# A backbone kernel on one core: the second layer's latent rows are loaded during the first layer's last expert, and that expert's rows are added to them on chip

## The chip, the cores and the metric

The kernel runs on one core of a Trainium2 chip. The metric is the device time of one execution in microseconds (us); lower is better.

## The reference

The model is a trunk of two layers over 512 latent rows and 256 context rows of 1024 numbers (float32). Each layer normalises and modulates its input, mixes it (attention, retention and a recurrence between an input and an output projection), adds the result to the residual, and then runs 16 experts. Each expert picks 64 latent rows and 32 context rows, and its results are added back to the rows that it picked. The second layer has no context output.

```python
    for i in range(DEPTH):                                   # DEPTH = 2
        ...
        hl = _modulate(_rms(xl, norm1_g[i]), sh1_l, sc1_l)
        hc = _modulate(_rms(xc, norm1_g[i]), sh1_c, sc1_c)
        mix_l, mix_c = _mixer(hl, hc, ...)                   # h @ w_in, heads, concat, @ w_out
        xl = xl + g1_l * mix_l
        xl = xl + g2_l * _expert_choice_ffn(_modulate(_rms(xl, norm2_g[i]), sh2_l, sc2_l), ...)
        if need_ctx:                                         # layer 0 only
            xc = xc + g1_c * mix_c
            xc = xc + g2_c * _expert_choice_ffn(...)
    return xl

def _expert_choice_ffn(h, router_w, w_gate, w_up, w_down):
    ...
    aff, idx = lax.top_k(jnp.swapaxes(probs, 1, 2), cap)     # each of 16 experts picks cap rows
    xs = h[bidx, idx]
    hid = jax.nn.silu(xs @ w_gate) * (xs @ w_up)             # per expert
    out = (hid @ w_down) * aff[..., None]
    return jnp.zeros_like(h).at[bidx, idx].add(out)
```

## The kernel before

`emit` (L1478) builds one program. For each layer it runs `mixer` (normalisation, input projection, heads), `outer` (output projection, residual, routing, gather of the first expert's rows) and `experts`, and then goes on to the next layer. The residual between the layers lies in DRAM, in `xr_l` (latent rows) and `xr_c` (context rows).

**The experts of layer 0.** `outer` writes the residual after the mixer to `xr_l` and `xr_c` (`base_write`). For each expert `gate_up` multiplies the gathered latent rows with two weight matrices (`gu`, L1304), `gate_up_c` does it for the context rows (`guc`, L1380), `down` (`oe`, L1457) and `down_c` (`oec`, L1470) multiply with the third, and `scatter` (L1403) adds the scaled results, `ob` (L1460) and `oc` (L1473), into `xr_l` and `xr_c` in DRAM by an indirect DMA on POOL's queue. `down_c` of an expert stands after `gate_up` of the next one; that of the last stands at the end of `experts`.

**The experts of layer 1** have latent rows only, and these are not scattered. The residual stays in SBUF; `onehot` (L1406) compares an `iota` row with the expert's indices (`oh`, L1409) and makes two copies of the result rows for the matmul (`obs`, L1415 on ACT, L1416 on DVE); `combine` (L1442) then multiplies the one with the other (`cb`, L1447), which puts each row at its place, and adds it to the residual (L1449).

**Between the layers.** After the last expert `mod_bulk` (L305) makes two of the next layer's modulation rows: four 2 MB tiles of `mod_w` are loaded (`mwt`, L314) and multiplied (`macc`, L317), the sums are added to `mrow` (L319), and the first row is turned (`mT`, L330) and copied into the columns `ab` (L339). Then layer 1's `load_x` (L375) loads four latent tiles `xl` and two context tiles `xc` of 512 KB each from `xr_l` and `xr_c` (L383). `norm1` (L386) squares them on ACT into a PSUM tile called `junk` (L398), scales them (L409 on DVE, L411 on ACT) and transposes them (`xT`, L420). The input projection loads its weights as `wraw` (L449, 512 KB), splits them into two parts `ws` (L456 on ACT, L457 on DVE) and multiplies with the split activations `hh` and `hl` (`pf`, `pt`, L462 to L464).

**What sets the order.** A tile scheduler orders the instructions of each engine; each engine then runs its list strictly in that order, and waits where an operand or a buffer is not ready. SP's queue carries nearly all loads, in a list of its own. The PE instructions of `experts` are kept in program order (`pe`, L1369). Expert weights, `mwt`, `xl` and `xc` share a ring of 2 MB buffers in three pools (`bigm`, `big` with 5, `bign`); a load waits until the tile that lay in its buffer has been used. PSUM tiles of one pool take its four banks in turn (`b`), so a new tile waits for the reader of the tile four places before.

```python
        xl = self.t("big", [4, D], "xl")                       # load_x
        for t, x in enumerate(xs):
            eng.dma_start(x, src_l[t * P:(t + 1) * P] if t < 4 else src_c[(t - 4) * P:(t - 3) * P])
        ...
        if ctx:
            late()                                             # experts: down_c of the last expert
        self.fixed = False
        if mn is not None:
            self.mod_bulk(mn, (2, 3))
```

Of the kernel before, what the change touches and what calls it, by code (L numbers as in the profile page):

```python
# [20 lines left out]
P = 128  # L21
L = 512
C = 256
T = L + C
D = 1024
KD = D // P
NE = 16
# [3 lines left out]
DEPTH = 2  # L31
# [36 lines left out]
class Trunk:  # L68
    def __init__(self, ctx, tc, a, out):
        self.tc = tc  # L70
        self.nc = tc.nc
        self.a = a
        self.out = out
        self.n = 0
        self.fl = 0
        self.nw = 0
        self.pools = {}
        self.late = []
        self.mj = 0
        self.fixed = False  # L80
        pool = lambda nme, **kw: ctx.enter_context(tc.tile_pool(name=nme, **kw))
        self.cp = pool("cst", bufs=1)
        self.sp = pool("small", bufs=2)
        self.dr = pool("dr", bufs=1, space=bass.MemoryType.DRAM)
        self.pools["big"] = pool("big", bufs=NBIG)
# [287 lines left out]
        return g2  # L373

    def load_x(self, src_l, src_c, eng, ctx=True):  # L375
        xl = self.t("big", [4, D], "xl")
        self.xt = [xl]
        xs = [xl[:, t] for t in range(4)]
        if ctx:
            xc = self.t("big", [2, D], "xc")  # L380
            xs += [xc[:, t] for t in range(2)]
        for t, x in enumerate(xs):
            eng.dma_start(x, src_l[t * P:(t + 1) * P] if t < 4 else src_c[(t - 4) * P:(t - 3) * P])  # L383
        return xs

# [728 lines left out]
    def route_(self, i, s, xs, lg, ssp, base):  # L1114
        nc = self.nc
# [31 lines left out]
        for t in range(nt):  # L1147
            h, u = divmod(t, nt // 2)
# [36 lines left out]
            nc.vector.tensor_copy(af[o], tt[:, 0])  # L1185
            nc.vector.tensor_scalar(sc[o], tt[:, 1], float(nq), float(q), op0=ALU.mult, op1=ALU.add)
        r = {"g": g, "af": af, "sc": sc}
        if i == DEPTH - 1:
            r["ix"] = self.cst([NE], nm="ixl")
            for q in range(nq):  # L1190
                nc.vector.tensor_copy(r["ix"][cap * q:cap * (q + 1)], tt[:, 1])
# [119 lines left out]
    def experts(self, i, m, mn, st, first, base_l, base_c):  # L1311
        nc = self.nc
        ctx = i < DEPTH - 1
        bl = base_l.rearrange("t (h e) -> (t h) e", h=2)
        bc = base_c.rearrange("t (h e) -> (t h) e", h=4) if ctx else None
        self.g2 = self.gate2(m, ctx)
        gl = lambda e: self.moe_gather(m, 0, self.xh_l[i], st[0]["g"][:, e // 2:e // 2 + 1])
        gc = lambda e: self.moe_gather(m, 1, self.xh_c, st[1]["g"][:, e // 4:e // 4 + 1])
        xl, W, hid = first
        if ctx:  # L1320
            xc = gc(0)()
        self.fixed = True
        late = None
        part = []
        if not ctx:
            self.iota = self.t("iota", [L], "iota")
            nc.sync.dma_start(self.iota, self.a["iota"])
        for e in range(NE):
            if e > 0:
                W = self.load_experts(i, e, 6 * e + 6)  # L1330
                hid = self.gate_up(e, W, xl)
            turn = []
            if e % 2 == 1 and e < NE - 1:
                turn.append(gl(e + 1))
            if ctx and e % 4 == 3 and e < NE - 1:
                turn.append(gc(e + 1))
            if late is not None:
                late()
            pair = len(part) == 2 or not ctx and e == NE - 1
            if pair:  # L1340
                self.combine(part, 0)
            self.turn_hid(hid)
            if turn:
                xl = turn[0]()
            if ctx:
                hc = self.gate_up_c(e, W, xc)
                if len(turn) > 1:
                    xc = turn[1]()
            elif pair:
                self.combine(part, 1)  # L1350
                part = []
            if not ctx and e == NE - 1:
                dd = self.keep_x((1, 3))
            ob = self.down(e, W, hid, st[0])
            if ctx:
                self.scatter(bl, ob, st[0], e)
                self.turn_hid_c(hc)
                late = lambda e=e, W=W, hc=hc: self.down_c(e, W, hc, st[1], bc)
            else:
                part.append(self.onehot(e, ob, st[0]))  # L1360
        if part:
            self.last(part[0], dd, base_l)
        if ctx:
            late()
        self.fixed = False
        if mn is not None:
            self.mod_bulk(mn, (2, 3))
# [110 lines left out]
def emit(ctx, tc, a, out):  # L1478
    k = Trunk(ctx, tc, a, out)
    k.consts()  # L1480
    ms = [k.mod_start(i) for i in range(DEPTH)]
    src = (a["x"], a["ctx"])
    for i in range(DEPTH):
        last = i == DEPTH - 1
        base = (out, None) if last else (k.xr_l, k.xr_c)
        with ExitStack() as cw:
            k.open(cw, k4=(NK4, 0))
            with ExitStack() as cr:
                k.open(cr, P=(2, 1), d=(2, 1), b=(2, 1))
                rr = cr.enter_context(ExitStack())  # L1490
                k.open(rr, "right", q2=(NQ2, 0), ring=(NRING, 0), w4=(NW4, 0), mw=(NMW, 0))
                with ExitStack() as ca:
                    k.open(ca, w6=(NW6, 0), st=(NST, 0), p=(NPT, 0))
                    xs, g1 = k.mixer(i, ms[i], None if last else ms[i + 1], src, src)
                k.open(cw, bigm=(NBIGM, 0), gathl=(1, 0), xsl=(2, 0))
                with ExitStack() as cb:
                    k.open(cb, x2=(NX2, 0), x1=(NX1, 0))
                    if not last:
                        k.open(cb, xc=(1, 0))

                    def free():
                        rr.close()
                        k.open(cw, "right", bign=(NBIGN[i], 0))

                    st, xl = k.outer(i, ms[i], xs, src[1], g1, free, *base)
            k.open(cw, ob=(2 if not last else 1, 0), g2=(2 if not last else 1, 0))
            if not last:
                k.open(cw, gathc=(1, 0), xsc=(2, 0), hidc=(2, 0), oc=(1, 0))
            else:
                k.open(cw, iota=(1, 0), oh=(2, 0), obs=(4, 0))  # L1510
            k.open(cw, b=(4, 1), d=(2, 1))
            k.experts(i, ms[i], None if last else ms[i + 1], st, xl, *base)
        src = base
# [91 lines left out]
```

## Time and profile before

| What | Value |
|---|---|
| Time, median of 3 runs (lowest to highest) | 1968.45 us (1968.3 to 1970.06) |
| Profiled execution, its own time | 1968.01 us |
| Its span, from first to last instruction | 1966.2 us |
| PE (matmul) busy | 1823.2 us, 93% |
| DVE busy | 869.5 us, 44% |
| ACT busy | 604.4 us, 31% |
| POOL busy | 94.1 us, 5% |
| DMA | 541.70 MB, mean 275 GB/s over the span |
| Mean granted TensorE clock | 0.98 of full speed |

Times in the trace count from the start of the span. The execution's own time is 1.8 us longer than its span. Layer 0's experts run from about 525 us to 1061 us, the passage to layer 1 lies between 1056 us and 1096 us, and layer 1's experts take the last quarter. A line of the timeline gives the start, the duration, the engine, the program line and the operation, with its output and inputs (`out<-in`); in brackets stands how long the engine had been idle before, and what released it.

### The profile page before, as it was taken

How to read it: one execution, taken by the hardware profiler on the slowest of the kernel's cores; microseconds unless marked ns; L12 is line 12 of the kernel's file. 1: busy time of each engine (PE TensorE's matmuls, PEld its weight loads, DVE VectorE, ACT ScalarE, POOL GpSimd, SP SyncE). 2: the span in 40 equal slices, each digit the busy share in tenths (PEclk: the TensorE clock that was granted, in tenths of full speed). 3: DMA queues.
4: the chain of work that ended last, by engine and by line, in shares of the span. 5: the costliest groups of instructions: out<-in, count | busy, mean ns of one | idle time of the engine just before them, and what ended most of it. 6: DMA issues, size and time to landing. Idle time of an engine off the chain costs nothing.

```text
span 1966.2 us, 28927 instructions
## 1 busy us (share of the span) xinstructions
PE 1823.2 (93%) x11972; PEld 1059.9 (54%) x11972; DVE 869.5 (44%) x2049; ACT 604.4 (31%) x1257; POOL 94.1 (5%) x102
## 2 busy tenths in 40 slices
PE   6999999999899999999997989999994998888887
PEld 5788888677533333333333779986671332332322
DVE  6797867575510111011101687976763221222212
ACT  5656456433210101011102485564431111110111
POOL 0000000000110111111001000000001000000000
PEclk9999999999999999999999999999996999999999
DMA  8453334236789999999999521111449999999996
GB/s 318 134 170 108 127 129 133 70 128 249 282 350 404 401 407 404 404 401 406 394 398 353 204 73 43 44 44 58 159 163 367 427 427 428 427 427 427 427 427 278
DMA packets 74148, 541.70 MB, mean 275 GB/s; under 512 B 8320, under 2 KB 14352, under 8 KB 49696
## 3 DMA queue, kind: packets, MB, share of 16 engines
q1 hardware_dynamic: 61408, 499.03, 63.6%
q0 software_dynamic: 12464, 40.69, 6.5%
q8 instruction: 94, 1.54, 0.3%
q14 instruction: 38, 0.31, 0.0%
q10 hardware_dynamic: 144, 0.13, 0.0%
HBM read 522.51 MB, written 17.30 MB: 275 GB/s over the span
## 4 chain that ended last, share of the span: by engine, by line
PE 66%; DMA 16%; DVE 8%; issue 7%; ACT 3%; POOL 0%; SPq 0%; ACTq 0%; POOLq 0%
PE gu L1304 16%; PE oe L1457 8%; DMA w<-wu 8%; DMA w<-wg 6%; PE guc L1380 6%; PE oec L1470 3%; PE ao L885 3%; PE pt L462 2%; PE pt L464 2%; PE pf L462 2%; PE pt L463 2%; PE pf L463 2%; PE pf L464 2%; PE macc L296 2%; PE ro L773 1%
## 5 line engine op out<-in xcount | busy, mean ns | idle before, releaser
L1304 PE MATMUL gu<-w,xsT 128*64 128x512 f32 x2048 | 461.0, 603 | 42.7 <-DMA w<-wu 21.9
L1304 PEld LDWEIGHTS gu<-w,xsT 128*64 128x64 f32 x2048 | 146.3, 139 | 340.5 <-issue 278.0
L1457 PE MATMUL oe<-w,hid 128*64 128x512 f32 x1024 | 226.8, 596 | 0.7 <-ACT hid L1393 0.7
L1308 DVE TENSOR_TENSOR hid<-hid,gu 128x512 f32<-128x512 f32 x32 | 21.9, 685 | 330.5 <-ACT hid L1307 330.5
L1307 ACT ACTIVATE hid<-gu 128x512 f32<-128x512 f32 x32 | 19.1, 597 | 458.8 <-PE gu L1304 447.1
L1457 PEld LDWEIGHTS oe<-w,hid 128*64 128x64 f32 x1024 | 70.7, 137 | 144.7 <-issue 139.2
L462 PE MATMUL pt<-ws,hh 128*128 128x256 f32 x448 | 129.4, 290 | 0.9 <-ACT qk L124 0.9
L463 PE MATMUL pt<-ws,hh 128*128 128x256 f32 x448 | 127.8, 286 | 0.6 <-DVE ws L457 0.5
L464 PE MATMUL pt<-ws,hl 128*128 128x256 f32 x448 | 127.1, 284 | 0.0
L1380 PE MATMUL guc<-w,xsT 128*32 128x512 f32 x1024 | 113.2, 594 | 0.2 <-ACT xsT L1270 0.2
L1449 DVE TENSOR_TENSOR xl<-xl,cb 128x512 f32<-128x512 f32 x68 | 42.3, 681 | 129.9 <-PE cb L1447 129.8
L456 ACT ACTIVATE ws<-wraw 128x256 fp32r<-128x256 f32 x192 | 73.2, 411 | 70.0 <-PE pt L464 24.8
L1460 DVE SCALAR_TENSOR_TENSOR ob<-oe,afl,g 128x512 f32<-128x512 f32 x32 | 24.0, 751 | 159.5 <-PE oe L1457 159.5
L462 PEld LDWEIGHTS pt<-ws,hh 128*128 128x128 f32 x448 | 85.4, 191 | 8.1 <-issue 6.6
L457 DVE TENSOR_TENSOR ws<-wraw,ws 128x256 fp32r<-128x256 f32 x192 | 76.4, 419 | 24.3 <-ACT ws L456 23.7
L463 PEld LDWEIGHTS pt<-ws,hh 128*128 128x128 f32 x448 | 85.6, 191 | 1.3 <-DVE ws L457 1.2
L464 PEld LDWEIGHTS pt<-ws,hl 128*128 128x128 f32 x448 | 85.6, 191 | 0.1
L863 ACT ACTIVATE p<-sc,mx 128x768 f32<-128x768 f32 (+1 forms) x80 | 65.1, 815 | 40.2 <-DVE mx L861 37.1
L462 PE MATMUL op<-ws,mh 128*128 128x256 f32 x256 | 73.0, 285 | 3.1 <-ACT mh L972 3.1
L463 PE MATMUL op<-ws,mh 128*128 128x256 f32 x256 | 72.4, 284 | 0.0
L464 PE MATMUL op<-ws,ml 128*128 128x256 f32 x256 | 71.8, 282 | 0.3 <-DVE ml L973 0.3
L861 DVE TENSOR_REDUCE mx<-sc 128x1 f32<-128x768 f32 (+1 forms) x80 | 66.2, 846 | 10.1 <-PE sc L857 9.5
(401 smaller groups left out, 3217.5 us busy)
## 6 DMA issues: line engine op xcount, KB each, us to landing
w<-wd SPq DMA_DIRECT2D x63, 2048.0 KB, 22.3
w<-wg SPq DMA_DIRECT2D x62, 2048.0 KB, 26.3
w<-wu SPq DMA_DIRECT2D x61, 2048.0 KB, 15.0
mw<-mod_w SPq DMA_DIRECT2D x64, 512.0 KB, 4.4
wraw<-w_in SPq DMA_DIRECT2D x48, 512.0 KB, 3.8
wo<-wo SPq DMA_DIRECT2D x24, 384.0 KB, 3.8
mw<-mod_a SPq DMA_DIRECT2D x16, 512.0 KB, 10.2
mwt<-mod_w SPq DMA_DIRECT2D x4, 2048.0 KB, 15.5
```

The lines of the kernel that those rows point to most:

```text
L456: nc.scalar.activation(t[:, 0], src, AF.Copy)
L457: nc.vector.tensor_tensor(t[:, 1], src, t[:, 0].bitcast(F32), op=ALU.subtract)
L462: nc.tensor.matmul(out, lh, rh, start=first, stop=False)
L463: nc.tensor.matmul(out, lh, rl, start=False, stop=False)
L464: nc.tensor.matmul(out, ll, rh, start=False, stop=last)
L861: nc.vector.tensor_reduce(mx, s[:, :n], axis=AX.X, op=ALU.max, negate=True)
L863: nc.scalar.activation(ptl[m][:, :n], s[:, :n], AF.Exp, bias=mx, accum_out=sm[:, m, t:t + 1])
L885: nc.tensor.matmul(ao, aT[:, kt * P:(kt + 1) * P], v6[:, vt, h * P:(h + 1) * P], start=kt == 0, stop=kt == n - 1)
L1304: self.pe(nc.tensor.matmul(d[64 * h:64 * h + 64, j, :], xl[:, k, x0:x0 + CAPL], W(j, k)[:, h * 512:(h + 1) * 512], start=k == 0, stop=k == ...
L1380: self.pe(nc.tensor.matmul(dc[32 * q:32 * q + 32, :], xc[:, k, c0:c0 + CAPC], W(q // 2, k)[:, (q % 2) * 512:(q % 2) * 512 + 512], start=k ...
L1457: self.pe(nc.tensor.matmul(o[64 * h:64 * h + 64, :], hid[:, 1, c * P + hh * 64:c * P + hh * 64 + 64], W(2, k)[:, h * 512:(h + 1) * 512], s ...
L1470: self.pe(nc.tensor.matmul(o[32 * q:32 * q + 32, :256], hc[:, x0:x0 + 32], W(2, k)[:, q * 256:(q + 1) * 256], start=k == 0, stop=k == KD - 1))
```

## The change

`experts` of layer 0 now takes a tile `pre` for the last expert (e = 15) and issues, ahead of `down`, the four loads of `xl` from `xr_l` on SP's queue. The scatters of experts 0 to 14 are in `xr_l` by then; that of expert 15 is not. `onehot` is called for expert 15, and after `late()` eight `combine` steps (4 row tiles by 2 halves) add that expert's rows to `pre`. The scatter of expert 15 into `xr_l` stays, because layer 1 reads `xr_l` a second time for its residual (POOL, L383). `load_x` of layer 1 uses `pre` and loads only `xc`. For this, `iota` is loaded in layer 0 too, and its indices `ixl` are made there (L1191). Line numbers of the changed kernel are higher by 1 to 13.

```diff
@@ -77,6 +77,7 @@
         self.pools = {}
         self.late = []
         self.mj = 0
+        self.pre = None
         self.fixed = False
         pool = lambda nme, **kw: ctx.enter_context(tc.tile_pool(name=nme, **kw))
         self.cp = pool("cst", bufs=1)
@@ -373,13 +374,16 @@
         return g2
 
     def load_x(self, src_l, src_c, eng, ctx=True):
-        xl = self.t("big", [4, D], "xl")
+        pre, self.pre = self.pre, None
+        xl = self.t("big", [4, D], "xl") if pre is None else pre
         self.xt = [xl]
         xs = [xl[:, t] for t in range(4)]
         if ctx:
             xc = self.t("big", [2, D], "xc")
             xs += [xc[:, t] for t in range(2)]
         for t, x in enumerate(xs):
+            if t < 4 and pre is not None:
+                continue
             eng.dma_start(x, src_l[t * P:(t + 1) * P] if t < 4 else src_c[(t - 4) * P:(t - 3) * P])
         return xs
 
@@ -1185,7 +1189,7 @@
             nc.vector.tensor_copy(af[o], tt[:, 0])
             nc.vector.tensor_scalar(sc[o], tt[:, 1], float(nq), float(q), op0=ALU.mult, op1=ALU.add)
         r = {"g": g, "af": af, "sc": sc}
-        if i == DEPTH - 1:
+        if s == 0:
             r["ix"] = self.cst([NE], nm="ixl")
             for q in range(nq):
                 nc.vector.tensor_copy(r["ix"][cap * q:cap * (q + 1)], tt[:, 1])
@@ -1322,9 +1326,8 @@
         self.fixed = True
         late = None
         part = []
-        if not ctx:
-            self.iota = self.t("iota", [L], "iota")
-            nc.sync.dma_start(self.iota, self.a["iota"])
+        self.iota = self.t("iota", [L], "iota")
+        nc.sync.dma_start(self.iota, self.a["iota"])
         for e in range(NE):
             if e > 0:
                 W = self.load_experts(i, e, 6 * e + 6)
@@ -1351,17 +1354,27 @@
                 part = []
             if not ctx and e == NE - 1:
                 dd = self.keep_x((1, 3))
+            if ctx and e == NE - 1:
+                self.pre = self.t("big", [4, D], "xl")
+                for t in range(4):
+                    nc.sync.dma_start(self.pre[:, t], base_l[t * P:(t + 1) * P])
             ob = self.down(e, W, hid, st[0])
             if ctx:
+                if e == NE - 1:
+                    part = [self.onehot(e, ob, st[0])]
                 self.scatter(bl, ob, st[0], e)
                 self.turn_hid_c(hc)
                 late = lambda e=e, W=W, hc=hc: self.down_c(e, W, hc, st[1], bc)
             else:
                 part.append(self.onehot(e, ob, st[0]))
-        if part:
+        if not ctx:
             self.last(part[0], dd, base_l)
         if ctx:
             late()
+            self.xt = [self.pre]
+            for t in range(4):
+                for h in range(2):
+                    self.combine(part, h, (t,))
         self.fixed = False
         if mn is not None:
             self.mod_bulk(mn, (2, 3))
@@ -1506,8 +1519,7 @@
             k.open(cw, ob=(2 if not last else 1, 0), g2=(2 if not last else 1, 0))
             if not last:
                 k.open(cw, gathc=(1, 0), xsc=(2, 0), hidc=(2, 0), oc=(1, 0))
-            else:
-                k.open(cw, iota=(1, 0), oh=(2, 0), obs=(4, 0))
+            k.open(cw, iota=(1, 0), oh=(1 if not last else 2, 0), obs=(2 if not last else 4, 0))
             k.open(cw, b=(4, 1), d=(2, 1))
             k.experts(i, ms[i], None if last else ms[i + 1], st, xl, *base)
         src = base
```

On SP's list the four loads of `xl` move from behind the four loads of `mwt` to ahead of them. They take the buffer that the first `mwt` had; each `mwt` has the buffer that the next one had before, and the first now waits, like the last one before, for expert 15's first `guc` matmuls. The load of `iota` stands ahead of the load of expert 1's second `wg` tile, and waits for the product with one of the last tiles of `wo`, in whose place it lies.

Three more places follow, row by row. In the names, the number at the end is that of the tile.

**DVE, end of layer 0's output projection** (`op` is its product, `tmp` the gated product, `xc` the context residual, `oh` the one-hot rows). Before:

```order
L966 TENSOR_TENSOR tmp_5623<-op_5606,g_771_4481 128x512
L968 TENSOR_TENSOR xc_5145<-xc_5145,tmp_5623 128x2x256
L126 COPY xT_996_5629<-xT_995_5626 128x256
L966 TENSOR_TENSOR tmp_5663<-op_5646,g_771_4481 128x512
L968 TENSOR_TENSOR xc_5145<-xc_5145,tmp_5663 128x2x256
L1091 COPY xT_1010_5675<-xT_1009_5672 128x256
```

and with the change:

```order
L970 TENSOR_TENSOR tmp_5626<-op_5609,g_771_4481 128x512
L972 TENSOR_TENSOR xc_5145<-xc_5145,tmp_5626 128x2x256
L127 COPY xT_997_5632<-xT_996_5629 128x256
L970 TENSOR_TENSOR tmp_5666<-op_5649,g_771_4481 128x512
L1422 TENSOR_SCALAR oh_8469<-iota_5923,ixl_5508 128x512
L972 TENSOR_TENSOR xc_5145<-xc_5145,tmp_5666 128x2x256
L1095 COPY xT_1011_5678<-xT_1010_5675 128x256
L1095 COPY xT_1013_5683<-xT_1012_5680 128x256
```

`oh` stands between the last `tmp` and the last addition to `xc`. It needs the landing of `iota`.

**PE, after the last expert** (`oec` is the last context product). Before:

```order
L1470 MATMUL oec_8457<-w_8315,hidc_8428 32x256 x16
L317 MATMUL macc_8495<-mwt_8496,scT_87 32x256 x16
L317 MATMUL macc_8495<-mwt_8514,scT_87 32x256 x16
L317 MATMUL macc_8536<-mwt_8537,scT_87 32x256 x16
L317 MATMUL macc_8536<-mwt_8555,scT_87 32x256 x16
```

and with the change:

```order
L1483 MATMUL oec_8484<-w_8329,hidc_8442 32x256 x16
L1460 MATMUL cb_8520<-obs_8471,oh_8469 128x512
L1460 MATMUL cb_8523<-obs_8474,oh_8469 128x512
L1460 MATMUL cb_8526<-obs_8471,oh_8469 128x512
L1460 MATMUL cb_8529<-obs_8474,oh_8469 128x512
L1460 MATMUL cb_8532<-obs_8471,oh_8469 128x512
L1460 MATMUL cb_8535<-obs_8474,oh_8469 128x512
L1460 MATMUL cb_8538<-obs_8471,oh_8469 128x512
L1460 MATMUL cb_8541<-obs_8474,oh_8469 128x512
L318 MATMUL macc_8546<-mwt_8547,scT_87 32x256 x16
L318 MATMUL macc_8546<-mwt_8565,scT_87 32x256 x16
L318 MATMUL macc_8587<-mwt_8588,scT_87 32x256 x16
```

Eight `cb` stand between `oec` and the first `macc`.

**ACT, the start of layer 1.** Before:

```order
L1400 ACTIVATE hidc_8428<-hTc_8451 128x256
L326 DMA gr_98<-mrow_8493 128x256
L398 ACTIVATE junk_8636,n1s_8633<-xl_8625 128x1024
L398 ACTIVATE junk_8640,n1s_8633<-xl_8625 128x1024
L157 ACT_TABLE_LOAD
L157 ACTIVATE warm_8638<-n1s_8633 128x1
L398 ACTIVATE junk_8642,n1s_8633<-xl_8625 128x1024
```

and with the change:

```order
L1413 ACTIVATE hidc_8442<-hTc_8478 128x256
L1428 ACTIVATE obs_8471<-ob_8467 64x512
L1428 ACTIVATE obs_8474<-ob_8467 64x512
L327 DMA gr_98<-mrow_8544 128x256
L460 ACTIVATE ws_8853<-wraw_8849 128x256
L402 ACTIVATE junk_8685,n1s_8682<-xl_8445 128x1024
L402 ACTIVATE junk_8689,n1s_8682<-xl_8445 128x1024
L158 ACT_TABLE_LOAD
L158 ACTIVATE warm_8687<-n1s_8682 128x1
```

The two `obs` are new, and one split of a weight, `ws`, moved from behind the squares and the scaling to ahead of the first square.

## Rows read from the trace of the kernel before

**Rows 1.** The page, part 4: the chain that ended last, share by engine.

```profile
PE 66%; DMA 16%; DVE 8%; issue 7%; ACT 3%; POOL 0%; SPq 0%; ACTq 0%; POOLq 0%
```

**Rows 2.** Stretches: length; busy of PE, PEld, DVE, ACT, POOL; PEclk; DMA share; GB/s.

```profile
514.00:516.00 2.00, 2.00 (x11) 1.11 (x10) 0.46 (x1) 0.00 (x0) 0.00 (x0) 1.00 0.00 0
560.00:700.00 140.00, 140.00 (x990) 50.92 (x991) 16.04 (x29) 14.55 (x29) 17.06 (x12) 1.00 0.98 388
1016.00:1046.00 30.00, 30.00 (x215) 10.67 (x211) 2.61 (x4) 2.17 (x4) 4.33 (x4) 1.00 1.01 394
1073.00:1086.00 13.00, 6.70 (x27) 5.16 (x27) 9.05 (x23) 11.33 (x24) 0.00 (x0) 0.50 0.74 297
1096.00:1106.00 10.00, 10.00 (x74) 7.71 (x77) 7.94 (x28) 8.32 (x22) 0.00 (x0) 1.00 0.82 285
```

**Rows 3.** The chain of waits in layer 1's experts, in order of time.

```profile
1679.90 37.87 DMA w<-wg
...
1717.83 39.08 DMA w<-wu
```

**Rows 4.** Timeline of the passage to layer 1, all engines.

```profile
1060.53 7.09 PE L317 MATMUL macc<-mwt,scT 128*32 128x256 f32 x128
1060.78 0.48 DVE L1473 SCALAR_TENSOR_TENSOR oc<-oec,afc,g 128x256 f32<-128x256 f32 x1 [3.79 <-PE oec L1470]
...
1062.96 2.23 SPq L383 DMA_DIRECT2D xl<-xr_l  x4
...
1066.76 5.38 SPq L449 DMA_DIRECT2D wraw<-w_in  x2
...
1068.64 0.24 DVE L339 COPY ab<-mT 128x8 f32<-128x8 f32 x2 [0.53 <-PE mT L330]
1069.05 1.03 ACT L398 ACTIVATE junk<-xl 128x1024 f32<-128x1024 f32 x1 [12.05 <-DVE ab L339]
...
1079.08 1.63 ACT L456 ACTIVATE ws<-wraw 128x256 fp32r<-128x256 f32 x5
...
1082.95 0.79 PE L462 MATMUL pf<-hh,ws 128*128 128x512 f32 x1 [1.40 <-ACT hh L444]
```

**Rows 5.** Waits of SP's queue, 1000 to 1060 us: total, times, longest.

```profile
SPq L383 <- DMA xr_l<-ob,sl: 16.7, 1, 16.7
```

**Rows 6.** Timeline of layer 0's output projection and routing, end.

```profile
510.15 5.35 PE L956 MATMUL op<-wo,mxc 128*128 128x256 f32 x24
...
515.54 0.69 DVE L966 TENSOR_TENSOR tmp<-op,g 128x512 f32<-128x512 f32 x1 [4.97 <-PE op L956]
516.26 0.69 DVE L968 TENSOR_TENSOR xc<-xc,tmp 128x512 f32<-128x512 f32 x1
...
517.10 0.63 PE L1088 MATMUL xT<-ident,xc 128*128 128x128 f32 x4 [1.05 <-DVE xc L968]
...
525.07 5.03 PE L1304 MATMUL gu<-w,xsT 128*64 128x512 f32 x10 [0.85 <-ACT xsT L1270]
```

**Rows 7.** The chain of waits at a lone `wraw` load, 140 to 150 us.

```profile
143.77 3.77 DMA wraw<-w_in
```

**Rows 8.** Layer 1's `iota` and `oh`: durations ns (min/median/max), issue to landing us.

```profile
L1409 DVE TENSOR_SCALAR oh<-iota,ixl x16: 469/479/623, 1494.3 to 1918.1; 128x512 fp32r<-128x512 f32 x16
...
DMA to landing us min/median/max: 18.8/18.8/18.8
```

**Rows 9.** Timeline of layer 1's first `onehot` and `combine`.

```profile
1552.11 1.28 ACT L1415 ACTIVATE obs<-ob 64x512 fp32r<-64x512 f32 x2 [4.55 <-DVE ob L1460]
...
1564.94 2.12 PE L1447 MATMUL cb<-obs,oh 128*128 128x512 f32 x8
1565.71 0.69 DVE L1449 TENSOR_TENSOR xl<-xl,cb 128x512 f32<-128x512 f32 x1 [11.53 <-PE cb L1447]
1566.91 4.27 DVE L1449 TENSOR_TENSOR xl<-xl,cb 128x512 f32<-128x512 f32 x7
```

**Rows 10.** The `mwt` loads: durations ns, first and last issue us; landing us.

```profile
L314 SPq DMA_DIRECT2D mwt<-mod_w x4: 368/373/385, 1017.1 to 1045.8; - x4
...
DMA to landing us min/median/max: 11.6/15.5/25.7
```

## Prediction

> **What bounds the kernel now.** The page's chain comes first [rows 1]: PE has 66% of it and DMA 16%, so the question for each stage is whether PE or the loads set its end. The stretches answer it for layer 0's experts [rows 2]: PE is busy for 140.00 of 140 us and 30.00 of 30, with the DMA share at 0.98 to 1.01. A load that lands early there gives nothing, and whatever delays the first `gu` delays every later product. In layer 1's experts the chain runs through 2 MB weight loads of 37 to 39 us each [rows 3]; that stream starts when layer 1's earlier work gives its buffers free, so a shift reaches the end there too. From 1096 us PE is full again [rows 2]. Two places are left where PE is not full and the change has instructions: the passage between the layers, and the end of layer 0's output projection.
>
> In the passage [rows 4] the reader should look at ACT. It starts the first square at 1069.05, after 12.05 us of idleness, and what released it is the copy of `ab` on DVE, not the load of `xl`. (The square's PSUM tile takes the bank of `mT`, which `ab` reads.) From there to the first `pf` at 1082.95 ACT works without a gap. The chain above `ab` is `oec`, four groups of `macc` (7.09 us for 128 matmuls, so 1.77 per `mwt`), `mrow`, `mT`, `ab`. The load of `xl` did wait 16.7 us on SP's queue for the scatter [rows 5], which is the wait that the change takes away. But `xl` was issued at 1062.96, and its first tile was not what the square waited for last. Its cover is the `macc` chain.
>
> **What is removed, at no gain.** Four loads leave SP's queue at 1062.96, and 2 MB leave the DMA engines there. They are read earlier, in the stretch where PE is full. Price there: nothing, as PE never waits for a load in it; if that cover were gone, 2.1 MB at 394 GB/s are 5.3 us. The load waits for the scatter of expert 14 and takes the buffer of the first `mwt`. So the four `mwt`, issued from 1017.1 to 1045.8 [rows 10], are all issued from about 1045.8: 8.4 MB at 394 GB/s are 21.3 us, and a lone load spends 2.4 us beyond its bytes (3.77 us for 0.52 MB [rows 7]). The last lands at about 1069.5.
>
> **What is added at the passage.** `onehot` on ACT and DVE (obs 1.28 us, `iota` compared long before) runs beside `oec`, 3.66 us before `macc`, so it is free. The scatter of expert 15 stays and is off the path. Then eight `cb` and eight additions stand between `oec` and `macc`. In layer 1 the first addition starts 0.77 us after the first `cb`, and seven take 4.27 us, 0.60 to 0.61 each [rows 9]. PE's share, 2.12 us, would be the whole price if PSUM had room; that is the lower bound. But `cb` and `macc` share four banks, and the first `macc` takes the bank of the fifth `cb`, so it waits for the fifth addition. The first addition can start when `oc` is done, 1060.78 + 0.48 = 1061.26; the fifth ends at about 1061.3 + 0.7 + 4 x 0.61 = 1064.4. So `macc` starts at about 1064.5 instead of 1060.53: **+4.0 us**. Third and fourth groups: the third ends at 1064.5 + 3 x 1.77 = 1069.8, the fourth starts there, and its tile landed at about 1069.5; nothing more is lost, by a narrow margin. Upper bound here: all eight additions, +5.8.
>
> One move adds to it. ACT's list now has a `ws` ahead of the first square. It needs `wraw`, whose load waits in SP's queue for the third group of `macc`, since it lies in that tile's place; before, it was issued at 1066.76, behind `xl` and `xc`. Now it goes at about 1070.0, needs 3.77 us with the queue nearly empty [rows 7], lands at 1073.8, and the split takes 0.33 (1.63 for five). All squares and scalings are queued behind it. So the first square starts at about 1074.2 instead of 1069.05: **+5.2 us**. `ab` alone, with `macc` 4.0 us late, would let it start at 1073.05. Bounds: +2.1 (PE's time alone, `ws` not late) to +8 (the split waits for `wraw` behind two late `xc` tiles). I take 5.2, since `xc` is issued before, at its scatter's landing, and has left the queue. TensorE's half clock (0.50, 1.2 GHz) from 1073 to 1086 [rows 2] follows a stretch in which PE had stood idle, and PE will idle as long; it moves with the rest.
>
> **What is added at the output projection.** The `oh` of expert 15 does not need the expert's result, only `iota` and the indices, and so the scheduler put it early: on DVE between the last `tmp` and the last addition to `xc`. `iota` lies where a `wo` tile lay, and is loaded only when PE has used that: 4 `op` of 0.22 us (5.35 for 24) before the last, at about 514.7 [rows 6]. Until then DMA moves nothing, 0 GB/s from 514 to 516 [rows 2], so the load is alone. It has half the bytes of the lone `wraw`: 0.26 MB fewer are 0.67 us at 394 GB/s, so it takes 3.1 at the least, and 3.77 at the most. It lands at 517.8 to 518.5; `oh` takes 0.48 [rows 8]; the addition that began at 516.26 begins at 518.3 to 519.0, 2.0 to 2.7 later. Behind it on DVE, PE and ACT stand the whole rest of routing up to the first `gu` at 525.07, each waiting for the one before [rows 6]. I take **+2.5 us**, nearer to the row as it stands. It then stays, as PE is full until 1056. Lower bound +1.5, if ACT's work behind has slack of half a us; upper +17.7, with layer 1's 18.8 us from issue to landing [rows 8], whose queue was full of expert weights, unlike here. The Trainium skill, "DMA: Bandwidth & Descriptors", section "Anatomy of one DMA — SWDGE (gpsimd) path", fits a transfer as about 2.0 us and its bytes at 436 GB/s. By that, an estimate, 0.26 MB would take 2.6 us, the delay would be 1.5 us and the sum 1.0 us lower; the row of the lone `wraw` [rows 7] is 0.6 us above the same rule (3.2 for 0.52 MB), and the rule is for loads that GpSimd issues, so the row decides.
>
> The two index copies `ixl`, some tenths of a us on DVE, lie beside `op`, for which DVE waits 4.97 us at the end. Layer 1's own `combine` and `iota` are unchanged.
>
> **Sum.** 1968.01 (the profiled execution) + 2.5 + 5.2 = 1975.7. The median of the runs shown is 0.44 higher, so the forecast is **1976.0 us**. A measurement of this kernel can tell about 0.2%, 3.9 us, from no change: the band is 1964.5 to 1972.4.
>
> **Rivals.**
> - *The load leaves the path and the time falls.* If the square waits for its operand only, ACT could start once the first tile's two additions are done, 1061.3 + 0.7 + 0.6 = 1062.6, 6.4 us earlier. With `iota` in time that is 1968.45 - 6.4 = 1962. The deciding point is whether the square starts before `ab` is copied. Against it: the release by `ab` [rows 4], and `ws` ahead of the square on ACT. Chance 0.06. The Trainium skill says the same as advice ("DMA: Bandwidth & Descriptors", "Rules for kernel authors"): issue a load early, compute, and wait late. The row shows that the wait ended elsewhere.
> - *Only the passage costs.* `iota` lands before the last `tmp`, because its load is let go earlier. Then 1968.45 + 5.2 = 1973.7. Against it: `wo`'s tile and 0 GB/s in that stretch. Chance 0.12.
> - *The change does little.* The latent rows are still read from `xr_l` twice, and 2 MB only move in time. If `ws` is not late and the additions overlap `macc`, +2.1 at the passage and +1.5 at the output projection, half of it lost in slack: 1970 to 1972. Chance 0.10.
> - *`iota` lands as slowly as in layer 1.* 1968.45 + 17.7 + 5.2 = 1991. Against it: the empty queue. Chance 0.04.
>
> **How the numbers follow.** The forecast has 0.68. Its own bounds, from 1.5 + 4.0 to 2.7 + 8 above the median, are 1974.0 to 1979.2. The highest of the runs shown is 1.6 above their median, which goes on top. With the second rival, and most of the third, the range is 1971 to 1980.5; it leaves out the first and the last and a part of the third. Faster by over 0.2%: the first rival, 0.06. Within 0.2%: the third and a little of the forecast, 0.13. Slower: 0.81.
>
> **What would show it.** Right: DVE's `oh` waiting for `iota` between `tmp` and `xc` at about 516.3 to 518.3, and the first `gu` at about 527.5; the first `macc` at about 1067 (1064.5 and the 2.5 from before) released by an `xl` addition; `ws` ahead of the square released by `wraw` at about 1076.5; the first `pf` near 1090.7. Wrong: a square that starts before `ab`; `gu` at 525; or a `macc` that waits for an `mwt`, which would mean that the moved load costs what I put at nothing.

## The result and the profile after

| | before | with the change |
|---|---|---|
| Time, median of 5 runs (lowest to highest) | 1968.3 us (1967.64 to 1970.06) | 1978.39 us (1977.31 to 1984.37) |
| Profiled execution, own time / span | 1968.01 / 1966.2 us | 1977.79 / 1976.0 us |

The ratio is 1.0055, with a 95% interval of 1.0044 to 1.0066: slower by 0.55%. A second set of five runs gave 1980.4 us, ratio 1.0057 (1.0043 to 1.007). The forecast was 1976.0 us in a range of 1971.0 to 1980.5.

The page's chain has hardly changed against [rows 1]. The kernel is bound as before, and the loss is local.

```profile
PE 65%; DMA 17%; DVE 8%; issue 7%; ACT 3%; POOL 0%; SPq 0%; ACTq 0%; POOLq 0%; DVEq 0%
```

The end of layer 0's output projection, with the change; it answers to [rows 6]:

```profile
515.73 0.33 SPq L1330 DMA_DIRECT2D iota<-iota  x1
...
517.46 0.69 DVE L970 TENSOR_TENSOR tmp<-op,g 128x512 f32<-128x512 f32 x1 [4.98 <-PE op L960]
518.48 0.49 DVE L1422 TENSOR_SCALAR oh<-iota,ixl 128x512 fp32r<-128x512 f32 x1 [0.32 <-DMA iota<-iota]
518.88 0.68 DVE L972 TENSOR_TENSOR xc<-xc,tmp 128x512 f32<-128x512 f32 x1
...
528.49 4.40 PE L1308 MATMUL gu<-w,xsT 128*64 128x512 f32 x10 [0.85 <-ACT xsT L1274]
```

`oh` does wait for `iota` between `tmp` and the last addition to `xc`. But the addition starts 1.42 us after `tmp`, where it had started 0.72 after it: 0.7 us are lost there, not 2.5. At the first `gu` it is 1.5 us (11.03 after `tmp`, 9.53 before), since from 521 to 524 us PE was granted 0.59 of its clock, and 1.00 in the same matmuls before (from 518 to 520 us). The first ten `gu` then take 4.40 us and not 5.03, which gives 0.6 back.

The passage, with the change; it answers to [rows 4]:

```profile
1058.90 0.46 PE L1412 MATMUL hTc<-ident,hidc 64*128 64x64 f32 x4
...
1063.43 3.57 PE L1460 MATMUL cb<-obs,oh 128*128 128x512 f32 x8
...
1063.97 4.87 DVE L1462 TENSOR_TENSOR xl<-xl,cb 128x512 f32<-128x512 f32 x8
...
1067.10 5.39 PE L318 MATMUL macc<-mwt,scT 128*32 128x256 f32 x96
...
1071.97 0.83 SPq L387 DMA_DIRECT2D xc<-xr_c  x2
1072.97 0.81 SPq L453 DMA_DIRECT2D wraw<-w_in  x2
...
1075.07 3.31 PE L318 MATMUL macc<-mwt,scT 128*32 128x256 f32 x32 [2.59 <-DMA mwt<-mod_w]
...
1079.28 0.42 ACT L460 ACTIVATE ws<-wraw 128x256 fp32r<-128x256 f32 x1 [18.18 <-DMA wraw<-w_in]
1079.41 0.24 DVE L340 COPY ab<-mT 128x8 f32<-128x8 f32 x2 [0.53 <-PE mT L331]
...
1079.82 1.03 ACT L402 ACTIVATE junk<-xl 128x1024 f32<-128x1024 f32 x1
...
1093.70 0.50 PE L466 MATMUL pf<-hh,ws 128*128 128x512 f32 x1 [1.69 <-ACT hh L448]
```

The third group of `macc` ends at 1072.49. The fourth then waits 2.59 us for the DMA, and its 32 matmuls take 3.31 us (1.77 before, within the row of 128). The granted clock was 1.00 for the first three groups and 0.57 for the fourth, mostly at the lower of its two levels (columns as in [rows 2]):

```profile
1067.10:1072.50 5.40, 5.38 (x96) 3.01 (x96) 2.19 (x7) 0.00 (x0) 0.00 (x0) 1.00 1.06 370
1072.50:1075.07 2.57, 0.00 (x0) 0.00 (x0) 0.00 (x0) 0.00 (x0) 0.00 (x0) 0.89 1.02 367
1075.07:1078.40 3.33, 3.31 (x32) 1.38 (x32) 0.00 (x0) 0.00 (x0) 0.00 (x0) 0.57 1.01 402
```

`ab` is copied by 1079.65, the split ends at 1079.70, and the square follows at 1079.82. Two chains end together: `mwt`, `macc`, `ab`, and `xr_c`, `xc`, `wraw`, `ws`. The chain of waits names only the second.

To compare executions, times are counted from marks of their own. The last `tmp` marks the output projection. `hTc` of expert 15, the transposition of its context product, marks the place up to which PE is full. From the last `tmp` to `hTc` the kernel before took 540.58 us and the changed one 541.44; from `hTc` to the first `pf` 26.83 and 34.80; from there to the end of the span 883.25 and 882.30. That is +0.9, +8.0 and -1.0. The remaining 1.9 us of the span's 9.8 lie ahead of the last `tmp` (515.54 and 517.46). The change adds only the two copies `ixl` there, from 508.92 on, and the pair of `op` at 506.84 is already 1.9 us late (504.91 before).

### The profile page after: what moved, and what is told of

Same layout as the page of the kernel before. It is cut to its first block, busy times and chain, and to the rows that moved or that the text cites. A ratio compares the mean times of both kernels' runs of the same rounds, so it can differ in the third digit from the quotient of the medians.

```text
span 1976.0 us, 28960 instructions
## 1 busy us (share of the span) xinstructions
PE 1825.9 (92%) x11980; PEld 1060.2 (54%) x11980; DVE 876.2 (44%) x2062; ACT 606.3 (31%) x1259; POOL 94.2 (5%) x102
## 4 chain that ended last, share of the span: by engine, by line
PE 65%; DMA 17%; DVE 8%; issue 7%; ACT 3%; POOL 0%; SPq 0%; ACTq 0%; POOLq 0%; DVEq 0%
PE gu L1308 16%; PE oe L1470 8%; DMA w<-wu 8%; DMA w<-wg 6%; PE guc L1393 6%; PE oec L1483 3%; PE ao L889 2%; PE pt L466 2%; PE pf L466 2%; PE pt L467 2%; PE pt L468 2%; PE pf L467 2%; PE pf L468 2%; PE macc L297 2%; PE ro L777 1%
## 5 line engine op out<-in xcount | busy, mean ns | idle before, releaser
L1462 DVE TENSOR_TENSOR xl<-xl,cb 128x512 f32<-128x512 f32 x76 | 47.0, 679 | 128.8 <-PE cb L1460 128.8
## 6 DMA issues: line engine op xcount, KB each, us to landing
mw<-mod_a SPq DMA_DIRECT2D x16, 512.0 KB, 10.5
```

Of the source, the lines that this page charges most:

```text
L1462: nc.vector.tensor_tensor(xx, xx, p, op=ALU.add)
```

## The experiments

The code of each edit is shown cut to the lines that matter, with comments added. Time ratios are against the kernel before, run beside each. The other columns are read from each profiled execution's timeline, in us; the fourth `macc`, `ab` and the first square are counted from `hTc`.

```
                     ratio (95% interval)     tmp-xc  tmp-hTc  4th macc    ab  square  hTc-pf
before               1                         0.72   540.58      9.7    12.5   12.9   26.83
change               1.0055 (1.0044, 1.0066)   1.42   541.44     16.2    20.5   20.9   34.80
change again         1.0057 (1.0043, 1.0070)   1.32   541.39     16.9    21.3   21.7   35.58
e1 oh late           1.0046 (1.0029, 1.0063)   0.73   540.84     16.5    21.1   21.5   35.40
e2 mwt ring          1.0045 (1.0028, 1.0061)   1.33   542.90     13.8    16.7   21.3   35.12
e3 combine last      1.0072 (1.0056, 1.0089)   1.30   541.37     16.9    21.3   26.6   40.62
e4 ws behind         1.0045 (1.0028, 1.0062)   1.28   541.04     16.0    20.6   21.0   34.94
e7 ring, ws behind   1.0025 (1.0016, 1.0035)   1.40   541.58     13.9    16.8   17.2   31.20
e8 = e7, no adding   1.0031 (1.0019, 1.0043)   1.43   541.20     14.5    19.4   19.9   33.83
e10 load only        1.0046 (1.0032, 1.0059)   0.72   541.03     16.2    20.5   20.9   34.79
e6 before, bank      1.0010 (1.0001, 1.0019)   0.72   540.91      9.7    12.5   11.0   25.52
e5 four edits        0.9988 (0.9979, 0.9997)   0.73   539.68     13.7    19.3    6.4   23.69
```

(The fourth `macc` of before, e5 and e6 has no wait; its start is the group's start and three quarters of its length.)

**e1, the one-hot rows late.**

```diff
-        nc.vector.tensor_scalar(oh, self.iota, st["ix"][:, e:e + 1], None, op0=ALU.is_equal)
+        with self.tc.issue_after(self.obi.ins) if late else nullcontext():   # obi: DVE's ob
+            nc.vector.tensor_scalar(oh, self.iota, st["ix"][:, e:e + 1], None, op0=ALU.is_equal)
```

> The changed kernel with one edit: the one-hot rows of expert 15 are made after that expert's result on DVE, so that no instruction of the output projection stands behind the load of iota. Stretches from the trace: from the last tmp of the output projection (515.54 before, 517.46 with the change) to the last hTc the kernel before takes 540.58 us and the changed one 541.44. Theory: the wait for iota costs 0.9 us, so this stretch returns to 540.6 and the passage from hTc to the first pf stays at 34.8 (26.8 before); the time falls by about 1 us. The prediction's own size, 2.5 us, would show as a fall of 2.5. Rival: iota costs nothing lasting and the 0.9 us are chance; then the stretch stays at 541.4.

Measured: `xc` follows `tmp` by 0.73 us again, the first `gu` by 9.54 us (9.53 before; 10.1 to 11.3 in the executions that keep the wait), and the stretch to `hTc` is 540.84. The seven executions of the table that keep the wait have 541.56 on average, the five without it 540.61. So the wait costs 0.6 to 0.7 us at `xc` and about 0.9 up to `hTc`, near what the theory had. The second figure holds as an average only: the two groups run from 541.04 to 542.90 and from 539.68 to 541.03, and this run alone gained 0.6. The time ratio does not resolve so little.

**e2, the ring of buffers advanced**, and **e4, the splits behind the squares.**

```diff
                 self.pre = self.t("big", [4, D], "xl")
+                self.nw += 1
```

```diff
-            nc.scalar.activation(t[:, 0], src, AF.Copy)
+            with self.tc.issue_after(self.sqi.ins):          # sqi: the last square
+                nc.scalar.activation(t[:, 0], src, AF.Copy)
```

> The changed kernel with one edit: after the tile for the early x is taken, the ring of weight buffers is advanced by one place, so that the first two mwt go to buffers that come free earlier (1040 and 1042 us before) and not to the one that comes free last. Theory A: the passage is 8.0 us longer (34.8 against 26.8) because the fourth mwt lands late, behind a gap in the DMA stream, and the macc after it then runs at half clock; the eight additions ahead of macc account for only 4 of it. Then the passage falls to about 31, the fourth macc follows the third without a wait, and the time falls by about 4 us. Theory B (the prediction's step): the split of wraw, queued ahead of the squares, sets the start of layer 1, and mwt only fills time beside it; then the passage stays above 33.

> The changed kernel with one edit: the splits of the input projection's weights are issued on ACT behind the last square. In the changed kernel's trace the split ends at 1079.70 and ab at 1079.65, so two chains end together. Theory A: nothing to gain alone, the passage stays at 34.8 within 0.5 and the squares are released by ab. Theory B (the split is the cause of a delay over ab): the passage falls by 1 us or more.

In e2 the first part of theory A came, and the gain did not. From e2's timeline:

```profile
1072.12 1.93 PE L318 MATMUL macc<-mwt,scT 128*32 128x256 f32 x32 [0.21 <-DMA mwt<-mod_w]
...
1075.07 0.24 DVE L340 COPY ab<-mT 128x8 f32<-128x8 f32 x2 [0.53 <-PE mT L331]
...
1079.26 0.42 ACT L460 ACTIVATE ws<-wraw 128x256 fp32r<-128x256 f32 x1 [18.74 <-DMA wraw<-w_in]
1079.58 1.01 ACT L402 ACTIVATE junk<-xl 128x1024 f32<-128x1024 f32 x1
```

The fourth `macc` waits 0.21 us, `ab` comes 3.8 us earlier (16.7 after `hTc`), and the square stands behind the split until `wraw` has landed. So theory B's step is true here. e4 takes the split away, and the square then waits for `ab`:

```profile
1078.10 1.03 ACT L402 ACTIVATE junk<-xl 128x1024 f32<-128x1024 f32 x1 [18.76 <-DVE ab L340]
```

The passage stays at 34.9, as theory A said. Each chain alone is long enough for the whole delay. In the second execution of the changed kernel and in e1, with the split where the change has it, ACT was done with the split first and waited 0.29 and 0.43 us more, for `ab`.

**e3, combine behind mod_bulk.** The call moves below `self.mod_bulk(mn, (2, 3))`.

> The changed kernel with one edit: the eight combine steps stand behind mod_bulk and not ahead of it. Theory A (late mwt): the first three macc start at once, 3.7 us earlier, but the fourth still waits for its tile at about 1075, so ab comes no earlier, and the additions, now behind it, make the passage about 1 us longer: 35 to 36.5. Theory C: the additions ahead of macc set the end of the passage; then it falls by about 4 us, to 31.

The fourth `macc` waited for its tile as late as ever, 16.9 after `hTc`, which speaks against theory C. The passage grew by 5.8, not by 1: the first square was released by the last of the eight additions, at 26.6, and `wraw` came later too. Its own tile needs only the first two additions; a PSUM bank shared with the last `cb` would explain the wait, which no run of this order shows. Theory A named the right wait and missed that one.

**e7, e2 and e4 together**, and **e8, e7 without the adding.**

```diff
             self.xt = [self.pre]
-            for t in range(4):
-                for h in range(2):
-                    self.combine(part, h, (t,))
```

> The changed kernel with the edits of e2 and e4 together. Alone, each left the passage at about 35. Theory: two chains end together at 1079.7 in the changed kernel, mwt to ab and xc to wraw to the first split; with both shortened the square follows ab, which e2 has 16.7 us after hTc, so the first square starts at 17.1 after hTc (20.9 with the change) and the passage falls to about 31; the time falls by 4 us against the change. Rival: the split is needed by the first pf anyway, and wraw lands as late as before; then the passage stays at 33 or more.

> As e7, and the eight matmuls and additions of combine are left out, so that expert 15's latent rows are missing from layer 1's input. This prices the additions ahead of macc. Prediction's step: 4.0 us; then the passage is 4 us shorter than in e7, about 27. Rival: behind the additions the DMA stream would hold macc anyway (the fourth mwt lands some 13 us after hTc); then it is 1 to 2 us shorter only.

e7 did what was expected: `ab` at 16.8, the square at 17.2, the passage 31.2, and the ratio down from 1.0055 to 1.0025. e8 was the surprise. From its timeline:

```profile
1061.42 5.36 PE L318 MATMUL macc<-mwt,scT 128*32 128x256 f32 x96
...
1071.53 3.64 PE L318 MATMUL macc<-mwt,scT 128*32 128x256 f32 x32 [4.75 <-DMA mwt<-mod_w]
```

Without the additions `macc` starts 3.8 us earlier after `hTc`, and the fourth group waits 4.75 us for its tile instead of 0.28. The tile came 0.7 us later than in e7, the group takes 3.64 us (1.93 in e7), and the passage is longer, 33.8. The granted clock of the idle stretch and of the group, in e8:

```profile
1066.80:1071.50 4.70, 0.00 (x0) 0.00 (x0) 0.00 (x0) 0.00 (x0) 0.00 (x0) 0.81 0.84 248
1071.50:1075.20 3.70, 3.64 (x32) 1.36 (x32) 0.00 (x0) 0.00 (x0) 0.00 (x0) 0.50 0.92 355
```

The clock fell to its lower level (0.50) while PE stood idle, and the group ran at it. In e7 it was 1.00 in the same group:

```profile
1072.00:1074.00 2.00, 1.93 (x32) 0.94 (x32) 0.00 (x0) 0.00 (x0) 0.00 (x0) 1.00 0.79 216
```

The additions cost nothing here: they fill a wait for the DMA.

**e10, the load only**, in the kernel before.

```diff
+            if ctx and e == NE - 1:
+                pre = self.t("big", [4, D], "xe")
+                for t in range(4):
+                    nc.sync.dma_start(pre[:, t], base_l[t * P:(t + 1) * P])
             ob = self.down(e, W, hid, st[0])
```

> The kernel before, with only the early load added: four loads of xr_l into a spare tile, ahead of the four mwt on SP's queue, and nobody reads the tile. No one-hot rows, no additions; layer 1 loads its x as before. Theory: what made the passage 8 us longer is the position of the load ahead of mwt, in the buffer that the first mwt had; then it comes here without any addition: the fourth macc waits for its tile until 14 to 16 us after hTc (9.8 before), and the first pf is at 34 us or more (26.8 before, 34.8 with the change). As e8 has no additions and a passage of 33.8, the additions should be missed little. Rival: the additions make it, and the load alone leaves the passage at 27 to 29.

From its timeline:

```profile
1038.81 1.75 SPq L1357 DMA_DIRECT2D xe<-xr_l  x4
...
1047.62 4.99 SPq L314 DMA_DIRECT2D mwt<-mod_w  x4
...
1062.35 3.64 PE L317 MATMUL macc<-mwt,scT 128*32 128x256 f32 x64
...
1067.98 1.93 PE L317 MATMUL macc<-mwt,scT 128*32 128x256 f32 x32 [1.99 <-DMA mwt<-mod_w]
...
1074.16 3.04 PE L317 MATMUL macc<-mwt,scT 128*32 128x256 f32 x32 [4.25 <-DMA mwt<-mod_w]
...
1078.85 1.03 ACT L398 ACTIVATE junk<-xl 128x1024 f32<-128x1024 f32 x1 [20.02 <-DVE ab L339]
```

This settles where the 8.0 us of the passage come from. With nothing but four loads ahead of `mwt`, the fourth `macc` starts at 16.2, the square at 20.9 and the first `pf` at 34.79: the changed kernel's numbers, with no addition and no `ws` ahead of a square. The ratio, 1.0046, is most of the change's.

How the load does it stands in the stretch from 1036 to 1048 us, before and with the change:

```profile
1036.00:1048.00 12.00, 12.00 (x134) 4.68 (x134) 1.17 (x2) 1.19 (x2) 2.79 (x3) 1.00 0.98 368
```

```profile
1036.00:1048.00 12.00, 12.00 (x124) 4.75 (x124) 1.17 (x2) 1.20 (x2) 2.80 (x3) 1.00 0.76 263
1048.00:1060.00 12.00, 11.53 (x80) 3.64 (x76) 1.44 (x2) 1.15 (x3) 0.00 (x0) 1.00 0.94 342
1060.00:1070.00 10.00, 9.52 (x128) 5.03 (x124) 6.68 (x14) 1.08 (x2) 3.21 (x2) 1.00 1.04 371
```

On SP's queue, with the change:

```profile
1040.50 1.75 SPq L1360 DMA_DIRECT2D xl<-xr_l  x4
1048.58 5.73 SPq L315 DMA_DIRECT2D mwt<-mod_w  x4
```

The DMA share falls from 0.98 to 0.76, because all four `mwt` wait on SP's queue for a buffer until 1048.58. Then 8.4 MB take until 1075.07, 26.5 us, or 317 GB/s; all transfers together ran at 342 to 371 GB/s in those stretches. e2 splits the delay: with an earlier buffer for the first `mwt` (issued at 1042.12) the fourth tile comes at 13.8 after `hTc` and not at 16.2, so waiting for the buffer makes 2.4 of the 6.5 us.

**e6, the kernel before with the squares in other PSUM banks**, and **e5, the same in the changed kernel with e1, e2 and e4.**

```diff
-                k.open(cr, P=(2, 1), d=(2, 1), b=(2, 1))
+                k.open(cr, P=(2, 1), **({"b": (2, 1), "d": (2, 1)} if last else {"d": (2, 1), "b": (2, 1)}))
```

> The kernel before, with only the PSUM order edit of e5: the squares no longer share a bank with mT. If ab alone held the first square at 1069.05, it now starts when the first xl tile has landed, 1062.96 plus 4.1, so 1067.1, and the passage falls by 1 to 2 us (26.8 to 25 or 26); the load of xl is then on the path and an early load is worth something. If the square is not released by ab but by something that the profile does not show, nothing changes.

> The changed kernel with four edits: one-hot rows late (as in e1), the ring advanced (as in e2), the splits behind the squares (as in e4), and in layer 1 the PSUM pool of the squares opened above that of b, so that the squares take banks that no copy of ab reads. Theory: this frees the square from ab, and the early load can pay at last: the first square follows the second addition, 6 to 7 us after hTc (23.7 with the change), and the first pf comes when the first splits are done, about 21 to 23 us after hTc (26.8 before, 34.8 with the change). Against the kernel before the time falls by 3 to 5 us, if PE can use the early start. Rival: the DMA stream of mwt and xc delays wraw and so the splits; then the passage stays at 26 or more and the time is that of before or worse.

In e6 the square started at 11.0, released by the landing of `xl` (`[10.09 <-DMA xl<-xr_l]`), and the passage fell by 1.3. So `ab` did hold the square of the kernel before, and `xl` came next, 2 us earlier. The kernel as a whole became no faster, and if anything slower (1.0010). The stretch after the passage shows a reason, for before and for e6:

```profile
1096.00:1104.00 8.00, 8.00 (x57) 6.42 (x57) 6.70 (x23) 6.36 (x17) 0.00 (x0) 1.00 0.77 259
```

```profile
1096.00:1104.00 8.00, 8.00 (x32) 6.96 (x31) 5.21 (x15) 6.51 (x18) 0.00 (x0) 0.64 0.56 180
```

PE is full in both, but e6 got 0.64 of the clock and 32 matmuls against 57. This execution of e6 took 1974.08 us, 2.1 above its median, so the row shows how the gain can be lost, and not how much of it as a rule.

In e5 the early load pays at last. The square follows its two additions 6.4 us after `hTc`, beside `macc`, and the first `pf` comes at 23.7, 3.1 earlier than before. At layer 1's first `gate` matmuls 1.4 us of this are left (73.5 against 74.9 after `hTc`). The time is 1967.86 us against 1969.22 in the same set, ratio 0.9988. It is the fastest version here, by little more than the measurement can tell. Against e6, which has the bank edit without the early load, it is faster by 0.2% (1972.02 us in the same set).

## Why the prediction was right, and where it was not

**What bounds the kernel: right.** Both delays stayed for the most part: PE was full behind the first, and of its 1.5 us at the first `gu` about 0.9 were left at `hTc`; the second shifted all of layer 1. From the first `pf` to the end little came back (1.0 us).

**The square is released by `ab`, not by `xl`: right.** [rows 4] showed it, and e6 shows it by moving the bank.

**"What is removed, at no gain": this is the step that failed.** It priced the move of 2 MB at nothing. It did say that the first `mwt` would lose its buffer and that all four would be issued from about 1045.8. But it let them land by 1069.5, "by a narrow margin". In the changed kernel the fourth tile let `macc` go at 1075.07. Less the 2.8 us by which `hTc` was late, that is 1072.3 on the old scale. The sum used 394 GB/s from [rows 2], and the stretch gave 317 for `mwt`, shared with scatters and other loads. So not 4.0 us from the additions but 6.5 us from the tile (the fourth `macc` at 16.2 instead of 9.7 after `hTc`), and 1.5 more from that group, nearly all by the lower clock (3.31 us; 1.93 in e7 at 1.00), make the 8.0. e10 shows it alone, without additions. The prediction's last paragraph had named this sign: a `macc` that waits for an `mwt`.

**The additions, +4.0: the mechanism was right, the charge was not.** The first `macc` did wait for the fifth addition (8.2 against 4.4 after `hTc`, so 3.8). But e8 and e10 show that this lies within the wait for the tile.

**The split ahead of the square: right as a wait, and no larger than the other.** It was put 1.1 us above `ab`. In the changed kernel both ended within 0.05 us; e2 shows the split deciding, e4 `ab`. `wraw` left almost when forecast, at 1072.97 (1070.0, and 2.8 for the later `hTc`), but took 6.2 us to land, not 3.77: the queue was not nearly empty. Two `xc` tiles had been issued 1.0 us ahead, and the fourth `mwt` was still landing. (In e2, where that tile had landed by 1072.12, `wraw` left at 1072.39 and still took 6.8 us.) `xc` was taken to leave at its old time, at the landing of the scatter into `xr_c`. That scatter now took 7.6 us from POOL's issue at 1064.33 to SP's at 1071.97 (4.3 before, 1061.55 to 1065.87), beside the full `mwt` stream. This is the prediction's upper bound of +8, a split behind two late `xc` tiles, which it set aside for 5.2.

**`iota`, +2.5: the mechanism was right, mis-sized.** It cost about 0.9 us up to `hTc` (e1). Two parts of the term were wrong. The issue came 1.73 us ahead of the last `tmp` (515.73, 517.46), where the prediction had it 0.84 ahead (514.7 and 515.54). And from issue to `oh` it took 2.75 us (to 518.48), where 3.1 to 3.77 were put down. The Trainium skill's rule ("DMA: Bandwidth & Descriptors", "Anatomy of one DMA — SWDGE (gpsimd) path") gave an estimate of 2.6 us. The trace's 2.75 us agrees with it within 0.15, although this load is on SP's queue; the row of `wraw` that was preferred was the worse guide.

**Why the total still came near.** Forecast +2.5 and +5.2; measured about +0.9 and +8.0. The two misses nearly cancel, which is luck. (The sum itself is 1976.1 with its 0.44, not 1976.0.) The 1.9 us ahead of the last `tmp` are chance: over twelve executions that `tmp` lay between 515.43 and 517.46, and in the second execution of the changed kernel at 516.17.

> The changed kernel once more, unaltered, to see how much of the 1.9 us by which its profiled execution was late at the last tmp of layer 0 (517.46 against 515.54), ahead of anything that the change moved, is chance: that tmp lies anywhere from 515 to 517.5, and the passage from hTc to the first pf at 34.8 again within 0.5.

The passage was 35.58 there, 0.8 off and not 0.5.

**The rivals.** The faster one (the load leaves the path) did not come, since the square waited for `ab` or the split. e5 frees the square from both, with the ring and the late one-hot rows besides, and gains 0.1%; how much of this each edit gives on top of the others no run shows. *Only the passage costs* had the right place for 8.0 of 8.9 us. *The change does little* fails with the 8.0 us, and *`iota` lands as slowly as in layer 1* with 2.75 us from issue to `oh`, not 18.8. The Trainium skill's advice to issue a load early ("DMA: Bandwidth & Descriptors", "Rules for kernel authors") paid here only in e5, beside the other edits.

## What to carry to other kernels

A load that is moved forward in a full DMA stream can push the loads behind it and take a buffer that one of them had, as here. Find the first of these that somebody waits for, and price the move by how much later that one lands, less its slack, and not by the moved load's own. Here the fourth `mwt` landed 10.5 us later (1072.3 on the old scale; before, it was issued at 1045.8 and landed 16.0 later, at 1061.8), and its slack was 4.1 us (it was needed at 1065.9). Where two chains end together, undoing either shows nothing; undo both before calling a cause cleared. And a wait that an added step seems to cause may be one that it only fills, which taking the step out shows at once.

## What the runs showed that was not expected

- Taking work out of PE made the passage longer: e8 against e7, 33.8 against 31.2 us, with the same loads. PE waited 4.75 us for the tile instead of 0.28 and lost its head start there; of the 2.6 us, 1.7 come from the lower clock that it then got and 0.7 from the later tile. The medians, 1976.34 and 1973.87 us, differ the same way.
- Issuing `mwt` itself became long: with the change the longest of the four issues held SP's queue 4.19 us (0.385 before, [rows 10]), with three 2 MB loads just ahead of it.
